# Two first-block mixers without accumulating weight transfers, and a second block whose gate columns run under its attention

## The chip, the core and the metric

The kernel runs on one core of a Trainium2 chip. Its engines are TensorE (PE, and PEld for its weight loads), VectorE (DVE), ScalarE (ACT), GpSimd (POOL) and SyncE (SP, which here only starts transfers). The metric is the device time of one execution in microseconds. Three runs of the kernel before took 3379.87, 3381.11 and 3383.58 us; the median is 3381.11 us.

## The reference

The program is two blocks in a row on one sequence of 1024 tokens of width 1024, in float32.

```
for i in range(2):                                   # first block
    hn = rmsnorm(h, norm1[i]);  z = hn @ w_in[i]
    u, (q, k, v) = z[:256], split(z[256:], 3)        # 12 heads of 64
    h = h + concat(pool_mixer(u), dilated_mixer(q, k, v)) @ w_out[i]
    h = h + square(relu(rmsnorm(h, norm2[i]) @ w_up[i])) @ w_down[i]
    h = h + sigmoid(rmsnorm(h, norm3[i]) @ w_gate[i]) * (p[i] @ w_ple[i])
x = rmsnorm(h, final_norm)

u = x @ w_in_2 + b_in_2                              # second block, 5632 columns
q, k, v, z_att, glu_a, glu_b, z_conv, g_att, g_conv = split(u)
att  = stick_breaking(q, k, v)                       # 8 heads of 64, causal
a_br = (att * silu(z_att)) @ w_att_proj
c    = silu(layer_norm(causal_conv31(glu_a * sigmoid(glu_b))))
c_br = (c * silu(z_conv)) @ w_conv_proj + b_conv_proj
y    = (sigmoid(g_att) * a_br + sigmoid(g_conv) * c_br) @ w_out_2
out  = layer_norm(2**0.25 * x + y)
```

The dilated mixer is attention in three groups of four heads with windows; stick-breaking attention needs, for every query, a running product over its keys.

## The kernel before, in words

Every product of two float32 matrices is made of three passes of reduced-precision matmuls: a matrix is held as a high part (`whi`, `xh`) and a low part (`wlo`, `xl`), and PE adds high times high, high times low and low times high (`mm_b`, L318, L320, L322; `project`, L502 to L504; `project_a`, L574 to L576). A weight tile of 128x1024 comes from memory into `wst` (SP queue, L213, a ring of three buffers) and is split in `split_w`. ACT copies it into `whi` (L294). The low part is made in one of two ways. With `by_dma` off, DVE subtracts: `wlo = wst - whi` (L299). With `by_dma` on, ACT writes `-whi` into `wlo` (L296) and a transfer on the POOL queue (L297) reads the weight from memory once more and adds it. In the kernel before, `by_dma` is on in the mixer of each of the first block's two layers (from the pooled columns to the first two output columns) and in the second block from the first keys on until the convolution is finished.

All weights come in the order of one list (`make_plan`); `stage` loads up to four entries ahead, `advance` splits up to two ahead. A "column" in what follows is one 128-wide output column of a 1024-deep product for all 1024 tokens: 8 slices of 6 matmuls with 512 columns, 48 matmuls.

Two streams of work run beside these columns as Python generators. After each slice `mm_b` calls `tick(1.3)`, after each two of `project` `tick(1.36)`, and a generator spawned with a period takes one step whenever so many ticks have gone by. The order of the instructions on each engine is fixed in this way when the program is built; each engine then works through its own queue in order.

In the first block's mixer the attention of a group (scores `S`, L666 and L669; exponentials `E` on ACT, L677; transposes `te`, L694, into `ET`; values `o`, L722 and L724) runs beside the projections of the next one. Queries and keys are rotated: DVE writes `sh` and `zq` or `za` (L516, L517), a small transfer on the POOL queue adds shifted rows (`za<-sh`, L519), ACT and DVE then make the key's parts `kS` (L543, L551).

In the second block, `stick` is the attention: 64 scores (4 head pairs, 4 blocks of queries, 2 heads, 2 halves) over 128 to 1024 keys. A score is matmuls `S` (L1352, L1354), a mask on DVE (L1357), sigmoids on ACT (L1358, L1359), a running product on DVE (L1361), and a product (L1362). Its weights are then transposed (`tw`, L1370), split (`wh` on ACT, `wl` on DVE, L1374) and multiplied with the values (L1389, L1391). `conv_all` is the convolution: 31 steps on DVE for each of four channel tiles (L1312, L1315), then a layer norm. `stick` has a period of 1.6 ticks, `conv_all` of 2.0. The columns beside them are the inputs of both, the gates of the attention branch (`gate(m)`, columns 28 to 35, whose sigmoids SP stores to `sad`), and `z_att` (12 to 15). Then come `w_att` with the stored gates fetched back on the POOL queue (`fetch_sa`) and `z_conv` (24 to 27), then `w_conv` with the gates of the convolution branch (36 to 43), one column in front of most of its eight halves, and the partial sums read back from `mgd`; last the output product `fin` (L1633).

Of the kernel before, what the change touches and what calls it, by code (L numbers as in the profile page):

```python
# [12 lines left out]
F32 = mybir.dt.float32  # L13
# [55 lines left out]
class K:  # L69
# [80 lines left out]
    def make_plan(self):  # L150
        p = []
        for i in range(DEPTH):
            p += [("w_u", i, 0), ("w_u", i, 1)]
            for g in range(3):
                for which in ((0, 1, 2) if g < 2 else (1, 0, 2)):
                    p += [("w_qkv", i, g, which, j) for j in range(2)]
            p += [("w_out", i, 0), ("w_out", i, 1), ("old", i, 0), ("old", i, 1)]
            for m in range(2, 8):
                p += [("w_out", i, m), ("old", i, m)]
            ups = [("w_up", i, m) for m in range(32)]  # L160
            p += ups[0:4]
            for c in range(8):
                if c < 7:
                    p.append(ups[4 * c + 4])
                p += [("w_down", i, c, mp) for mp in range(4)]
                p += ups[4 * c + 5:4 * c + 8]
            for m in range(8):
                if m == 4:
                    p.append(("w_ple", i, 1))
                p.append(("w_gate", i, m))  # L170
                if m == 1:
                    p.append(("w_ple", i, 0))
        w2 = lambda *cs: [("w_in2", c) for c in cs]
        wv = lambda c: [("w_v", c, 0), ("w_v", c, 1)]
        p += w2(20, 16, 0, 4, 1) + wv(0) + w2(5, 28, 21, 17, 29, 2, 6, 30, 22, 18, 31) + wv(1) + w2(3, 7, 32, 23, 19, 33)
        p += w2(12, 13, 14, 15, 34, 35)
        for m in range(8):
            if m % 2 == 0:
                p.append(("w_att", m // 2))
            if m % 2 == 1:  # L180
                p += w2(24 + m // 2)
        p += w2(36, 37)
        wo = lambda *ks: [("w_out2", k) for k in ks]
        for m in range(8):
            if 0 < m < 7:
                p += w2(37 + m)
            if m % 2 == 0:
                p.append(("w_conv", m // 2))
            p.append(("mg", m))
            p += {5: wo(0), 6: wo(1), 7: wo(2, 3, 4, 5, 6, 7)}.get(m, [])  # L190
        return p

    RAW = ("old", "mg", "w_out2")
# [197 lines left out]
    def setup(self):  # L391
        nc, a = self.nc, self.a
        self.ident = self.const("ident", [128, 128])
        nc.sync.dma_start(self.ident, a["c_ident"])
        self.ones = self.const("ones", [128, 2])
        nc.vector.memset(self.ones, 1.0)
        self.qlow = [self.const("ql%d" % n, [128, 512], F32R) for n in range(2)]
        self.qn = 0
        for x in self.qlow:
            nc.gpsimd.memset(x.bitcast(F32), 0.0)  # L400
        self.pinv = self.const("pinv", [128, 34])
        nc.gpsimd.dma_start(self.pinv, a["c_pinv"])
        self.pscale = self.const("pscale", [128, 4])
        nc.gpsimd.dma_start(self.pscale, a["pool_scale"])
        self.td = self.dram.tile([2, 128, 1024], F32, name="td")
        self.xd = self.dram.tile([8, 128, 1024], F32, name="xd")
        self.mgd = self.dram.tile([8, 128, 1024], F32, name="mgd")
        self.sad = self.dram.tile([8, 128, 1024], F32, name="sad")
        self.atd = self.dram.tile([4, 128, 1024], F32, name="atd")
        self.od = self.dram.tile([2, 2, 128, 1024], F32, name="od")  # L410
        self.yd = self.dram.tile([2, 128, 1024], F32, name="yd")
        self.sd1 = self.dram.tile([128, 64], F32, name="sd1")
        self.sd23 = self.dram.tile([128, 128], F32, name="sd23")
# [466 lines left out]
    def mixer(self, i, nm, h):  # L880
# [31 lines left out]
        if i == 0:  # L912
# [1 line left out]
            next(self.rot)  # L914
            self.defer(2.6, lambda: next(self.rot, None))
            tabs, self.tabs = self.tabs, None
        self.by_dma = True
        self.defer(3.9, start)
        if i > 0:
            for k in range(8):  # L920
# [118 lines left out]
        part(us, pss, order[4:6])  # L1039
        part(us, pss, order[6:8])  # L1040
        self.drop(2)
        self.by_dma = False
        for m in range(2):
            out(m, pss[m])
        for m in range(2, 8):
# [141 lines left out]
    def second(self, nm, h):  # L1187
# [15 lines left out]
        def lin(col):  # L1203
            ps = self.pair("l2")
            self.gemm(("w_in2", col,), box["xs"], ps)
            return ps, bcol[:, col:col + 1]
# [6 lines left out]
        def sig_of(ps, b):  # L1213
            t = self.st("sg")
            nc.scalar.activation(t, ps, AF.Sigmoid, bias=b)
            return t
# [39 lines left out]
        def gate(m):  # L1256
            t = sig_of(*lin(28 + m))
            nc.sync.dma_start(self.sad[m], t)

        def glu(sg, src, b):  # L1260
            nc.vector.scalar_tensor_tensor(sg, src, b, sg, OP.add, OP.mult)
            return sg

        cvs = [None] * 4
        cg = [None] * 4
# [40 lines left out]
        def conv_all():  # L1306
            for j in range(4):
                while cg[j] is None:
                    yield
                C, cg[j] = cg[j], True  # L1310
                acc = cvs[j] = self.st("cv")
                nc.vector.tensor_scalar(acc, C, cw[:, j, 30:31], cb[:, j:j + 1], OP.mult, OP.add)  # L1312
                yield
                for d in range(1, 31):
                    nc.vector.scalar_tensor_tensor(acc[:, d:1024], C[:, 0:1024 - d], cw[:, j, 30 - d:31 - d],  # L1315
                                                   acc[:, d:1024], OP.mult, OP.add)
                    yield
                C = None
            for _ in conv_norm():
                yield  # L1320
# [168 lines left out]
        self.by_dma = True  # L1489
        q1 = queries(*lin(1))  # L1490
        vs[0] = values(0)
        sk = self.spawn(stick(), 1.6)
        qk[1] = (q1, keys(*lin(5)))
        gate(0)
        ca = self.spawn(conv_all(), 2.0)
        cg[1] = glu(sig_of(*lin(21)), *lin(17))
        gate(1)
        qk[2] = (queries(*lin(2)), keys(*lin(6)))
        gate(2)
        cg[2] = glu(sig_of(*lin(22)), *lin(18))  # L1500
        gate(3)
        vs[1] = values(1)
        qk[3] = (queries(*lin(3)), keys(*lin(7)))
        gate(4)
        cg[3] = glu(sig_of(*lin(23)), *lin(19))
        gate(5)
        zs, ats, aT = [], [], []
        for j in range(4):
            zs.append(silu_of(*lin(12 + j)))
        self.finish(sk)  # L1510
        for j in range(3):
            aT.append(self.st("aT"))
# [5 lines left out]
            aT[j] = None  # L1518
            ats.append(self.split(zs[j], "at"))

        att(0)
        att(1)
        gate(6)
        att(2)
        att(3)
        gate(7)
        zc, sas = [], []

        def fetch_sa(m):
# [5 lines left out]
        for m in range(8):  # L1535
            if m % 2 == 0:
                u = self.take("w_att", m // 2)
            if m < 6:
                fetch_sa(m + 2)
            ps = self.pair("pt")  # L1540
            self.mm_b(self.halves(ps), self.wk(u, 4, (m % 2) * 512), ats)
            sa, sas[m] = sas[m], None
            nc.vector.tensor_tensor(sa, ps, sa, OP.mult)  # L1543
            nc.sync.dma_start(self.mgd[m], sa)
            if m % 2 == 1:
                self.drop()
                zc.append(silu_of(*lin(24 + m // 2)))

        zs = zc
        self.finish(ca)  # L1550
# [3 lines left out]
        for j in range(4):  # L1554
            nc.vector.tensor_tensor(zs[j], zs[j], cvs[j], OP.mult)
            cts.append(self.split(zs[j], "ct"))
        gs = [sig_of(*lin(36 + m)) for m in range(2)]
        mg, ms = [], []
        xrs = {}

# [21 lines left out]
        def split_m(k):  # L1582
# [1 line left out]
            mg[k] = None  # L1584

        before = {5: [(split_m, 0)], 6: [(split_m, 2), (split_m, 3)], 7: [(scale_x, 0), (scale_x, 1), (split_m, 5)]}
        after = {5: [(split_m, 1), (split_wo, 0)], 6: [(split_m, 4), (split_wo, 1)],
                 7: [(split_wo, 2), (split_m, 6), (split_wo, 3), (split_m, 7), (split_wo, 4), (split_wo, 5),
                     (split_wo, 6), (split_wo, 7)]}
        for m in range(8):  # L1590
            if 0 < m < 7:
                gs.append(sig_of(*lin(37 + m)))
            sc = gs.pop(0)
            if m % 2 == 0:
                u = self.take("w_conv", m // 2)
            old = self.take("mg", m)
            ps = self.pair("pc")
            self.mm_b(self.halves(ps), self.wk(u, 4, (m % 2) * 512), cts)
            if m % 2 == 1:
                self.drop()  # L1600
            if m == 4:
                fetch(0)
                fetch(1)
            if m == 6:
                box["xs"] = None
            for f, k in before.get(m, []):
                f(k)
            nc.vector.scalar_tensor_tensor(sc, ps, cb[:, 12 + m:13 + m], sc, OP.add, OP.mult)
            nc.vector.tensor_tensor(sc, sc, old, OP.add)
            mg.append(sc)  # L1610
            for f, k in after.get(m, []):
                f(k)
# [215 lines left out]
```

## Time and profile before

| What | Value |
|---|---|
| median of three runs | 3381.11 us |
| the profiled execution: time, span | 3376.4 us, 3374.6 us |
| PE busy | 3234.1 us (96%) |
| DVE, ACT, POOL busy | 1716.5, 1188.5, 253.9 us |
| mean granted TensorE clock | 0.986 of full speed |
| read from and written to memory | 216.09 MB, 30.08 MB |

The busy time of PE is that of a pipelined engine: it counts the time in which a matmul is under way, so short gaps and a slow start behind a wait are hidden in it. What a stretch could take at best is better counted in matmuls times the pace of a stretch without waits. The first layer's mixer lies between about 30 and 375 us, the second layer's between about 1280 and 1620 us; the second block begins at about 2510 us, its attention runs from about 2598 to 3025 us.

### The profile page before, as it was taken

The numbers are of one execution on the slowest core, as the hardware profiler recorded it, in microseconds if no ns is written. First come the engines' busy times: TensorE is split into PE (matmuls) and PEld (weight loads), VectorE is DVE, ScalarE is ACT, GpSimd is POOL, SyncE is SP. The second block draws the span as 40 slices with busy tenths as digits, with TensorE's granted clock in tenths as the row PEclk, the third lists the DMA queues.
The fourth block names the chain that finished last, engine by engine and source line by source line (L and its number), as shares of the span: only waits on it lengthen the run. The fifth ranks groups of instructions, "written<-read, shape, count | busy, mean of one in ns | idle before, by whom it ended". The sixth has DMA issues, their size and how long they took to land.

```text
span 3374.6 us, 38172 instructions
## 1 busy us (share of the span) xinstructions
PE 3234.1 (96%) x15596; PEld 2695.1 (80%) x15596; DVE 1716.5 (51%) x2518; ACT 1188.5 (35%) x1914; POOL 253.9 (8%) x344
## 2 busy tenths in 40 slices
PE   8898999999999999989999999999999888889998
PEld 7787788888888887878788888888888767678887
DVE  6545643333333545555543333333656888886345
ACT  4666421111111323666331111112334554543230
POOL 5122000000000002123000000000000000001000
PEclk9899999999999999989999999999999999999999
DMA  5243321111111114323321111112113323226331
GB/s 178 63 89 81 89 82 45 50 50 50 45 49 57 57 50 138 85 66 90 91 75 50 45 50 48 47 50 65 44 44 114 82 59 75 74 65 199 109 122 63
DMA packets 74222, 251.79 MB, mean 75 GB/s; under 512 B 11280, under 2 KB 11456, under 8 KB 74048
## 3 DMA queue, kind: packets, MB, share of 16 engines
q1 hardware_dynamic: 49248, 174.44, 16.0%
q0 software_dynamic: 23504, 70.46, 9.9%
q10 hardware_dynamic: 1296, 4.46, 0.3%
q8 instruction: 123, 2.02, 0.2%
q14 instruction: 51, 0.42, 0.0%
HBM read 216.09 MB, written 30.08 MB: 73 GB/s over the span
## 4 chain that ended last, share of the span: by engine, by line
PE 73%; DVE 14%; ACT 6%; DMA 3%; issue 3%; POOL 1%; DVEq 0%; ACTq 0%; POOLq 0%
PE pu L320 7%; PE pu L322 7%; PE pu L318 7%; PE pd L320 7%; PE pd L322 7%; PE pd L318 7%; DVE cv L1315 3%; PE fin L1633 3%; PE l L318 2%; PE l L320 2%; PE l L322 2%; PE pg L318 2%; PE pg L322 2%; PE pg L320 2%; DMA za<-sh 2%
## 5 line engine op out<-in xcount | busy, mean ns | idle before, releaser
L294 ACT ACTIVATE whi<-wst 128x1024 fp32r<-128x1024 f32 x258 | 271.0, 1051 | 650.0 <-PE pd L320 497.3
L318 PE MATMUL pu<-xh,whi 128*128 128x512 f32 x1088 | 336.7, 391 | 9.2 <-ACT xh L60 9.2
L1111 DVE TENSOR_TENSOR h<-pd,h 128x1024 f32<-128x1024 f32 x128 | 156.6, 1224 | 365.6 <-PE pd L322 365.4
L320 PE MATMUL pu<-xl,whi 128*128 128x512 f32 x1088 | 335.8, 390 | 0.9 <-DVE xl L61 0.9
L322 PE MATMUL pu<-xh,wlo 128*128 128x512 f32 x1088 | 335.4, 389 | 0.0
L320 PE MATMUL pd<-hidl,whi 128*128 128x512 f32 x1024 | 315.4, 389 | 0.5 <-DVE hidl L307 0.5
L322 PE MATMUL pd<-hidh,wlo 128*128 128x512 f32 x1024 | 315.3, 389 | 0.0
L318 PE MATMUL pd<-hidh,whi 128*128 128x512 f32 x1024 | 315.2, 389 | 0.0
L299 DVE TENSOR_TENSOR wlo<-wst,whi 128x1024 fp32r<-128x1024 f32 x184 | 224.0, 1221 | 50.2 <-ACT whi L294 50.2
L1066 DVE SCALAR_TENSOR_TENSOR hid<-pu,bc 128x1024 f32<-128x1024 f32 x62 | 75.9, 1225 | 339.1 <-PE pu L322 338.9
L318 PEld LDWEIGHTS pu<-xh,whi 128*128 128x128 f32 x1088 | 204.1, 188 | 51.5 <-ACT xh L60 9.6
L1067 ACT ACTIVATE hid<-hid 128x1024 f32<-128x1024 f32 x62 | 65.7, 1060 | 508.7 <-DVE hid L1066 508.7
L320 PEld LDWEIGHTS pu<-xl,whi 128*128 128x128 f32 x1088 | 204.4, 188 | 44.6 <-DVE xl L61 2.1
L322 PEld LDWEIGHTS pu<-xh,wlo 128*128 128x128 f32 x1088 | 204.5, 188 | 42.6
L320 PEld LDWEIGHTS pd<-hidl,whi 128*128 128x128 f32 x1024 | 192.0, 188 | 41.0 <-DVE hidl L307 1.3
L318 PEld LDWEIGHTS pd<-hidh,whi 128*128 128x128 f32 x1024 | 192.2, 188 | 40.0
L322 PEld LDWEIGHTS pd<-hidh,wlo 128*128 128x128 f32 x1024 | 192.2, 188 | 39.9
L318 PE MATMUL l<-nh,whi 128*128 128x512 f32 x576 | 188.0, 408 | 0.3 <-DVE sa L1543 0.3
L502 PE MATMUL pa<-xh,whi 128*128 128x512 f32 x448 | 185.4, 414 | 0.0
L503 PE MATMUL pa<-xl,whi 128*128 128x512 f32 x448 | 180.4, 403 | 0.0
L320 PE MATMUL l<-nl,whi 128*128 128x512 f32 x576 | 180.4, 394 | 0.0
L504 PE MATMUL pa<-xh,wlo 128*128 128x512 f32 x448 | 180.0, 402 | 0.0
(353 smaller groups left out, 6028.6 us busy)
## 6 DMA issues: line engine op xcount, KB each, us to landing
wst<-in_w_up_dram SPq DMA_DIRECT2D x64, 512.0 KB, 3.5
wst<-in_w_down_dram SPq DMA_DIRECT2D x64, 512.0 KB, 3.5
wst<-in_w_in_dram SPq DMA_DIRECT2D x40, 512.0 KB, 4.8
wst<-in_w_qkv_dram SPq DMA_DIRECT2D x36, 512.0 KB, 4.1
wlo<-in_w_qkv_dram POOLq DMA_DIRECT2D x32, 512.0 KB, 8.2
wlo<-in_w_in_dram POOLq DMA_DIRECT2D x29, 512.0 KB, 5.7
wst<-in_w_out_dram SPq DMA_DIRECT2D x24, 512.0 KB, 3.7
wst<-in_w_gate_dram SPq DMA_DIRECT2D x16, 512.0 KB, 3.7
```

Of the source, the lines that this page charges most:

```text
L294: nc.scalar.activation(h, w, AF.Copy)
L299: nc.vector.tensor_tensor(l, w, h.bitcast(F32), OP.subtract)
L318: mm(ps[h], wh, xh[:, h * 512:(h + 1) * 512], start=st, stop=False)
L320: mm(ps[h], wh, xl[:, h * 512:(h + 1) * 512], start=False, stop=False)
L322: mm(ps[h], wl, xh[:, h * 512:(h + 1) * 512], start=False, stop=sp)
L502: mm(out, wh, xh, start=k == 0, stop=False)
L503: mm(out, wh, xl, start=False, stop=False)
L504: mm(out, wl, xh, start=False, stop=k == 7)
L1066: nc.vector.scalar_tensor_tensor(t, ps, 0.0, box["bc"], OP.max, OP.mult)
L1111: nc.vector.tensor_tensor(h[m], ps, h[m], OP.add)
L1315: nc.vector.scalar_tensor_tensor(acc[:, d:1024], C[:, 0:1024 - d], cw[:, j, 30 - d:31 - d], acc[:, d:1024], OP.mult, OP.add)
L1633: nc.tensor.matmul(ps[e], xx[:, tok], ww[:, cs], start=False, stop=k == 7 and ww is wh and xx is ml, skip_group_check=True)
```

## The change

Two things are changed. In the mixers the switch `by_dma` stays off, so that the 38 weight tiles that were split there by ACT and an accumulating transfer are split by ACT and a subtraction on DVE. In the second block the columns stand in another order: the eight gate columns of the convolution branch are no longer computed inside the `w_conv` loop; seven of them (36 to 42) run beside or just behind the attention and are stored to `sad` like the others, the keys and queries of a head pair come later, `z_att` stands behind the attention, and the periods are 1.85 ticks for `stick` and 2.60 for `conv_all`.

```diff
@@ make_plan
-        p += w2(20, 16, 0, 4, 1) + wv(0) + w2(5, 28, 21, 17, 29, 2, 6, 30, 22, 18, 31) + wv(1) + w2(3, 7, 32, 23, 19, 33)
-        p += w2(12, 13, 14, 15, 34, 35)
+        p += w2(20, 16, 0, 4, 1) + wv(0) + w2(28, 21, 17, 29, 30, 31, 5, 32, 22, 18) + wv(1) + w2(2, 6, 33, 34, 35, 23, 19)
+        p += w2(3, 7, 36, 37, 38, 39, 40, 41, 12, 13, 14, 15, 42)
...
-            if 0 < m < 7:
-                p += w2(37 + m)
...
@@ mixer
-        self.by_dma = True
...
-        self.by_dma = False
@@ second
-        sk = self.spawn(stick(), 1.6)
+        sk = self.spawn(stick(), 1.85)
+        gate(0)
+        ca = self.spawn(conv_all(), 2.60)
+        cg[1] = glu(sig_of(*lin(21)), *lin(17))
+        for m in (1, 2, 3):
+            gate(m)
         qk[1] = (q1, keys(*lin(5)))
-        gate(0)
-        ca = self.spawn(conv_all(), 2.0)
...
-        gate(5)
+        for m in range(8, 14):
+            gate(m)
         zs, ats, aT = [], [], []
-        for j in range(4):
-            zs.append(silu_of(*lin(12 + j)))
         self.finish(sk)
...
-        att(0)
-        att(1)
-        gate(6)
-        att(2)
-        att(3)
-        gate(7)
+        for j in range(4):
+            zs.append(silu_of(*lin(12 + j)))
+            att(j)
+        gate(14)
...
-            if m < 6:
-                fetch_sa(m + 2)
+            fetch_sa(m + 2)
...
-        gs = [sig_of(*lin(36 + m)) for m in range(2)]
+        gs = sas[8:10]
+        g7 = sig_of(*lin(43))
...
         for m in range(8):
-            if 0 < m < 7:
-                gs.append(sig_of(*lin(37 + m)))
+            if m < 4:
+                fetch_sa(m + 10)
+                gs.append(sas[m + 10])
+            if m == 4:
+                fetch_sa(14)
+                gs += [sas[14], g7]
```

What the change does to the queues is seen at three places. First ACT in the first mixer, behind the first four exponentials of an attention group. Before:

```order
L677 ACTIVATE E,stat_378<-E,stat_378 128x128 x4
L294 ACTIVATE whi<-wst 128x1024
L296 ACTIVATE wlo<-whi 128x1024
L294 ACTIVATE whi<-wst 128x1024
L296 ACTIVATE wlo<-whi 128x1024
L650 ACTIVATE qS<-zq 64x256 x4
L543 ACTIVATE kS<-za 64x512 x2
```

Now, on ACT at the same place, and then on DVE at the same place:

```order
L675 ACTIVATE E,stat_378<-E,stat_378 128x128 x4
L292 ACTIVATE whi<-wst 128x1024 x2
L648 ACTIVATE qS<-zq 64x256 x4
L541 ACTIVATE kS<-za 64x512 x2
L675 ACTIVATE E,stat_378<-E,stat_378 128x256 x4
```

```order
L673 ISA E,stat_378<-S,bmasks 128x128
L673 ISA stat_378 128x1
L297 TENSOR_TENSOR wlo<-wst,whi 128x1024 x2
L651 SCALAR_TENSOR_TENSOR ql_142<-zq,qS 64x256 x2
L549 TENSOR_TENSOR kS<-za,kS 64x512 x2
```

Two copies have left ACT's queue in front of the queries `qS`, and two subtractions stand in DVE's queue in front of the queries' low part `ql`.

Second DVE in the second block, between two of the longest scores of the first head pair (`S` the mask, `fP` the running product, `be` the product, `cv` steps of the convolution). Before:

```order
L1357 TENSOR_TENSOR S_18136<-S_18136,smask 128x128
L1361 SCALAR_TENSOR_TENSOR fP<-fP 128x1024
L1362 TENSOR_TENSOR be<-be,fP 128x1023
L1315 SCALAR_TENSOR_TENSOR cv<-sg,n_16975,cv 128x1017
L1374 TENSOR_TENSOR wl<-tw,wh 128x384
L1315 SCALAR_TENSOR_TENSOR cv<-sg,n_16975,cv 128x1016
L1357 TENSOR_TENSOR S_18177<-S_18177,smask 128x128
```

Now:

```order
L1353 TENSOR_TENSOR S_18128<-S_18128,smask 128x128
L1357 SCALAR_TENSOR_TENSOR fP<-fP 128x1024
L1358 TENSOR_TENSOR be<-be,fP 128x1023
L1311 SCALAR_TENSOR_TENSOR cv<-sg,n_16937,cv 128x1012
L1370 TENSOR_TENSOR wl<-tw,wh 128x384
L1353 TENSOR_TENSOR S_18179<-S_18179,smask 128x128
```

One convolution step has gone from between these two scores; the longer periods leave fewer of them between scores on average and more matmuls of columns on PE.

Third SP's queue around the `w_conv` loop (`mgd` the stored partial sums, `w_in` a gate column, `w_out` the output weights). Before:

```order
L213 DMA wst<-mgd 128x1024
L213 DMA wst<-in_w_in_dram 128x1024
L213 DMA wst<-mgd 128x1024
L213 DMA wst<-in_w_in_dram 128x1024
L213 DMA wst<-in_w_conv_dram 128x1024
L213 DMA wst<-mgd 128x1024
L213 DMA wst<-in_w_in_dram 128x1024
L213 DMA wst<-mgd 128x1024
```

Now:

```order
L1537 DMA mgd<-sa 128x1024 x4
L211 DMA wst<-mgd 128x1024 x2
L211 DMA wst<-in_w_conv_dram 128x1024
L211 DMA wst<-mgd 128x1024 x2
L211 DMA wst<-in_w_conv_dram 128x1024
L211 DMA wst<-mgd 128x1024 x2
```

The loads of the partial sums and of `w_conv` follow each other without the weights of a gate column between them.

## Rows read from the trace of the kernel before

**Rows 1.** The page, part 1: busy time of each engine.
```profile
PE 3234.1 (96%) x15596; PEld 2695.1 (80%) x15596; DVE 1716.5 (51%) x2518; ACT 1188.5 (35%) x1914; POOL 253.9 (8%) x344
```
**Rows 2.** Busy time by stretch: length, PE, PEld, DVE, ACT, POOL, clock, DMA share, GB/s.
```profile
480.00:520.00 40.00, 40.00 (x178) 33.12 (x177) 17.28 (x16) 13.92 (x14) 0.00 (x0) 1.00 0.14 45
...
80.00:400.00 320.00, 286.71 (x1679) 248.32 (x1678) 178.45 (x473) 192.43 (x448) 67.75 (x94) 0.95 0.34 80
...
1320.00:1640.00 320.00, 291.91 (x1696) 252.40 (x1696) 175.53 (x470) 189.46 (x445) 69.48 (x97) 0.94 0.34 79
...
2598.00:3047.00 449.00, 397.47 (x2077) 324.33 (x2078) 384.92 (x488) 236.25 (x449) 23.35 (x28) 0.98 0.30 72
...
3047.00:3265.00 218.00, 217.69 (x969) 179.60 (x968) 95.51 (x96) 61.60 (x60) 14.51 (x19) 1.00 0.45 131
```
**Rows 3.** PE's waits over the whole span: us in total, times, longest.
```profile
PE S L666 <- ACT E L677: 19.5, 4, 5.6
PE te L694 <- DVE ET L704: 11.0, 6, 2.8
PE S L666 <- DVE kS L551: 10.1, 10, 5.4
```
**Rows 4.** ACT in order of time before one wait for E: start, us, instruction.
```profile
1445.84 1.04 ACT L294 ACTIVATE whi<-wst 128x1024 fp32r<-128x1024 f32 x1
1446.92 1.06 ACT L296 ACTIVATE wlo<-whi 128x1024 fp32r<-128x1024 f32 x1
...
1449.92 1.72 ACT L650 ACTIVATE qS<-zq 64x256 fp32r<-64x256 f32 x4
```
**Rows 5.** DVE at the same place, in order of time.
```profile
1450.36 0.42 DVE L653 SCALAR_TENSOR_TENSOR ql<-zq,qS 64x256 fp32r<-64x256 f32 x1 [8.60 <-ACT qS L650]
```
**Rows 6.** The chain that ended last, first mixer: start, us, what.
```profile
75.52 1.78 POOL wlo L297
77.36 6.68 DMA za<-sh
...
88.32 2.38 DMA za<-sh
```
**Rows 7.** PE by form, 2575 to 3050 us: busy, mean ns, idle before.
```profile
L318 PE MATMUL l<-nh,whi 128*128 128x512 f32 x368 | 123.4, 417 | 0.0
...
L1370 PE MATMUL tw<-ident,be 128*128 128x128 f32 x208 | 33.6, 281 | 21.1 <-ACT be L1359 9.8 <-DVE wl L1374 7.7 <-DVE aT L1400 2.9
```
**Rows 8.** DVE by form, 2575 to 3050 us.
```profile
L1374 DVE TENSOR_TENSOR wl<-tw,wh 128x512 fp32r<-128x512 f32 x48 | 32.9, 686 | 3.9 <-ACT wh L1373 3.6
...
L1361 DVE TENSOR_TENSOR_SCAN fP<-fP 128x1024 f32<-128x1024 f32 x8 | 18.3, 2292 | 5.3 <-ACT fP L1358 5.3
...
L1361 DVE TENSOR_TENSOR_SCAN fP<-fP 128x640 f32<-128x640 f32 x8 | 11.9, 1493 | 2.8 <-ACT fP L1358 2.8
...
L1362 DVE TENSOR_TENSOR be<-be,fP 128x1023 f32<-128x1023 f32 x8 | 9.8, 1225 | 0.8
...
L1362 DVE TENSOR_TENSOR be<-be,fP 128x639 f32<-128x639 f32 x8 | 6.6, 825 | 0.8
...
L1315 DVE SCALAR_TENSOR_TENSOR cv<-sg,n,cv 128x1010 f32<-128x1010 f32 x4 | 5.1, 1264 | 0.0
```
**Rows 9.** DVE in order of time: masks of a head pair's eight long scores.
```profile
2731.58 0.29 DVE L1357 TENSOR_TENSOR S<-S,smask 128x128 f32<-128x128 f32 x1
...
2776.31 0.28 DVE L1357 TENSOR_TENSOR S<-S,smask 128x128 f32<-128x128 f32 x1
```
**Rows 10.** The page, part 5: DVE subtractions for low parts, whole span.
```profile
L299 DVE TENSOR_TENSOR wlo<-wst,whi 128x1024 fp32r<-128x1024 f32 x184 | 224.0, 1221 | 50.2 <-ACT whi L294 50.2
```
**Rows 11.** Transfers by line: KB each, median us from issue to landing.
```profile
sa<-sad POOLq DMA_DIRECT2D x8, 512.0 KB, 9.8
...
wst<-mgd SPq DMA_DIRECT2D x8, 512.0 KB, 3.5
```
**Rows 12.** PE waits of a mixer's late transposes, in order of time.
```profile
315.12 0.63 PE L694 MATMUL te<-ident,E 128*128 128x128 f32 x4 [2.78 <-DVE ET L704]
```

More of the change, by code (lines that the diff above doesn't have):

```diff
@@ L179, in make_plan @@
                 p.append(("w_att", m // 2))
-            if m % 2 == 1:
-                p += w2(24 + m // 2)
-        p += w2(36, 37)
+            if 0 < m < 5:
+                p += w2(23 + m)
+        p += w2(43)
         wo = lambda *ks: [("w_out2", k) for k in ks]
         for m in range(8):
-            if 0 < m < 7:
-                p += w2(37 + m)
             if m % 2 == 0:
@@ L189, in make_plan @@
             p.append(("mg", m))
-            p += {5: wo(0), 6: wo(1), 7: wo(2, 3, 4, 5, 6, 7)}.get(m, [])
+            p += {6: wo(0), 7: wo(1, 2, 3, 4, 5, 6, 7)}.get(m, [])
         return p
@@ L407, in setup @@
         self.mgd = self.dram.tile([8, 128, 1024], F32, name="mgd")
-        self.sad = self.dram.tile([8, 128, 1024], F32, name="sad")
+        self.sad = self.dram.tile([15, 128, 1024], F32, name="sad")
         self.atd = self.dram.tile([4, 128, 1024], F32, name="atd")
@@ L1491, in second @@
         vs[0] = values(0)
-        sk = self.spawn(stick(), 1.6)
+        sk = self.spawn(stick(), 1.85)
[4 more added lines that the diff above has]
+            gate(m)
         qk[1] = (q1, keys(*lin(5)))
-        gate(0)
-        ca = self.spawn(conv_all(), 2.0)
-        cg[1] = glu(sig_of(*lin(21)), *lin(17))
-        gate(1)
+        gate(4)
+        cg[2] = glu(sig_of(*lin(22)), *lin(18))
+        vs[1] = values(1)
         qk[2] = (queries(*lin(2)), keys(*lin(6)))
[L1499 to L1502, printed above, removed]
+        for m in (5, 6, 7):
+            gate(m)
+        cg[3] = glu(sig_of(*lin(23)), *lin(19))
         qk[3] = (queries(*lin(3)), keys(*lin(7)))
-        gate(4)
-        cg[3] = glu(sig_of(*lin(23)), *lin(19))
-        gate(5)
+        for m in range(8, 14):
+            gate(m)
         zs, ats, aT = [], [], []
-        for j in range(4):
-            zs.append(silu_of(*lin(12 + j)))
         self.finish(sk)
@@ L1546, in second @@
                 self.drop()
-                zc.append(silu_of(*lin(24 + m // 2)))
+            if 0 < m < 5:
+                zc.append(silu_of(*lin(23 + m)))
         zs = zc
@@ L1586, in second @@
         before = {5: [(split_m, 0)], 6: [(split_m, 2), (split_m, 3)], 7: [(scale_x, 0), (scale_x, 1), (split_m, 5)]}
-        after = {5: [(split_m, 1), (split_wo, 0)], 6: [(split_m, 4), (split_wo, 1)],
-                 7: [(split_wo, 2), (split_m, 6), (split_wo, 3), (split_m, 7), (split_wo, 4), (split_wo, 5),
+        after = {5: [(split_m, 1)], 6: [(split_m, 4), (split_wo, 0)],
+                 7: [(split_wo, 1), (split_wo, 2), (split_m, 6), (split_wo, 3), (split_m, 7), (split_wo, 4), (split_wo, 5),
                      (split_wo, 6), (split_wo, 7)]}
         for m in range(8):
-            if 0 < m < 7:
-                gs.append(sig_of(*lin(37 + m)))
+            if m < 4:
[4 more added lines that the diff above has]
+                gs += [sas[14], g7]
             sc = gs.pop(0)
```

## The prediction

> **What bounds the kernel now.** I read the busy times first: PE is busy for 96% of the span and the next engine for 51% [rows 1]. That makes PE the engine whose work sets the time, but not at its best everywhere, so the next view is busy time by stretch. In a stretch of the first MLP PE never waits: 178 matmuls in 40 us, 0.2247 us each, at a granted clock of 1.00, which is 2.4 GHz [rows 2]. One column of 48 matmuls is then 10.8 us. The change removes no matmul. What it can give is only time in which PE waits or starts slowly, and that lies in three stretches: the two mixers (33 and 28 us without a matmul in 320 us each) and the attention of the second block, 2598 to 3047 us (51.5 us without one) [rows 2]. From 3047 to 3265 us PE is busy to 0.3 us [rows 2].
>
> In the attention stretch the busy time hides more. PE's need there: 23 columns (368 matmuls in each of the three passes [rows 7]), 248 us; the products for the second half of the values, 192 matmuls half as wide, 22 us; the attention's own work. Scores and values each move 64 scores' worth, 73,728 columns of moving data, which at 0.2247 us for 512 is 32 us for either, and 288 transposes at about 0.11 us (half a 256-wide matmul's pace, an estimate) are 31 us. Together 366 us in 449 us: 83 us are lost. DVE is busy for 385 of the 449 us [rows 2], so it is the engine that PE waits for. The gaps between long scores show how: the masks of one head pair's eight long scores lie 6.39 us apart on average (44.73 us over 7) [rows 9]. In such a gap DVE has the mask 0.29 us, the running product 1.89 us and the product 1.03 us (means of the longest and the shortest form), a split `wl` 0.69 us, and, with two attention steps of 1.6 ticks and a convolution step each 2.0 ticks, 1.6 convolution steps of 1.26 us, 2.0 us [rows 8, 9]; with about 0.2 us for queries and sums that is 6.1 us, 95% of the gap. PE needs 3.2 ticks of columns, 3.2/1.3 times 6 matmuls, 3.3 us, and some 1.6 us of attention: 4.9 us. So PE loses 1.5 us at each of 32 long scores, 48 of the 83 us.
>
> **The change in the second block.** Seven gate columns of the convolution branch come into the stretch, and 76 us leave the loops behind it. The stretch then needs 442 us of PE. DVE's work in it stays about the same, because sigmoids of gates are ACT's. With 1.85 and 2.60 ticks a gap of two attention steps holds 3.7/1.3 times 6 matmuls, 3.85 us, and the 1.6 us of attention: 5.45 us for PE; DVE has 1.42 convolution steps, 1.8 us, and 5.9 us in all. At the same 95% the gap takes 6.2 us, and PE loses 0.75 us instead of 1.5: 24 us saved over 32. The other 35 us (short scores, ends of head pairs, waits for the clock) I lower by the ratio of what PE has to do in a gap, to about 25. So 83 us of loss become 48: minus 35 us. The bounds: nothing, if the loss stays whatever stands beside it, and 83 us, if PE never waits. A worse loss than before has no row for it: no DVE work is added there, and the later keys only hold up the attention, beside which gate columns run.
>
> **The w_conv loop.** It loses its gate columns, and 8 halves of 24 matmuls take 43 us. With column 43 in front, 54 us must cover what comes in: 8 partial sums, 3 tiles of `w_conv`, 5 stored gates, some 4 of `w_out`, 2 of x, 22 transfers of 512 KB, 11.5 MB, 213 GB/s. The stretch had 131 GB/s [rows 2]. Behind the ring of three buffers a partial sum's load waits for the sum two halves earlier and has 10.8 us less two DVE steps; a load takes 3.5 us there, but a fetch of a gate behind others on POOL took 9.8 us [rows 11]. I take plus 3 us. The near bound is 0; the far one is the loop at the rate of [rows 2], 11.5 MB at 131 GB/s, 88 instead of 54 us, plus 34. The same DVE chain that ends the convolution (four products, four splits at about 3.5 us each, 15 us behind the last `w_att`) now has 10.8 us of one column as its cover instead of two columns; the halves use the four tiles 1.35 us apart, which leaves at most 1 us of this, within the 3.
>
> **The mixers.** Each of the two loses 19 negated copies on ACT (1.06 us [rows 4]) and 19 transfers, and gains 19 subtractions on DVE at 1.22 us [rows 10], 46 us of DVE in all. DVE is busy 178 and 176 of 320 us there [rows 2].
>
> First, the waits for E: 4 times, 19.5 us in all [rows 3]. Before each of them ACT works through two tiles, `whi` and `wlo` twice, from 1445.84 to 1449.92, and the queries, whose low part DVE needs, come behind that [rows 4]; DVE has stood idle for 8.60 us at that point [rows 5], so two subtractions, which can begin when the first `whi` is there, end before `ql` can start. ACT comes to the queries 2.1 us earlier and the whole chain to E moves by that: 4 times 2.1, minus 8.4 us. Second, in each mixer the late transposes wait for the split `ET`, 2.78 us in the first [rows 12], 11.0 us over 6 waits [rows 3]; two tiles' copies stand in front of it on ACT, and in the order of now the two subtractions in front of it on DVE, which leave 1.7 of the 2.1 us: minus 3.4 us for both mixers. Third, the rotations' small transfers shared the POOL queue with the accumulating ones: behind two of them `za<-sh` was issued late (POOL 1.78 us) and took 6.68 us, where it takes 2.38 us otherwise [rows 6]. The key's parts then come 4 us or more earlier, but PE is still busy with its projection at that time, so that only the part of the 10.1 us of waits for kS [rows 3] that hangs on DVE's order goes: I take 1.2 us in each mixer and 0.8 us for later rotations, minus 4 us. Together minus 16 us. The bounds: all three kinds of waits gone, minus 40.6 us, and all subtractions in the path, 38 times 1.22, plus 46 us.
>
> What is queued behind the added wait: a subtraction waits for its `whi`, and `ql`, `ET`, `vS` or `kS` behind it on DVE wait too, and then PE. I see it covered in all ten places but expect no gain in six of them. The weight buffer is held until DVE has read it, some 2 to 5 us longer; loads run four entries ahead, a group of two tiles lasts over 20 us, and a load takes under 5 us.
>
> **The sum.** 3376.4 (the profiled execution) minus 35 minus 16 plus 3 is 3328.4 us. That execution lies 4.7 us under the median of the runs shown, so against the median I predict 3333 us.
>
> **Rivals.**
> - All of PE's loss in the attention goes: minus 83 instead of minus 35, 3285 us. For it: PE's need and DVE's are nearly equal in a long gap now. Against: the row of steps from score to scan to transposes stays, and DVE's 5.9 us still lie above PE's 5.45.
> - The attention's loss stays at 83 us because it is the chain's and not the load's: 3368 us. For it: DVE is at 86% over the stretch, not at 100% [rows 2]. Against: 95% in the long gaps.
> - The `w_conv` loop is held by its transfers, plus 34 instead of plus 3: 3364 us. For it: nothing stands between the loads any more, and fetched gates came in 9.8 us [rows 11]. Against: each gate is asked for two halves ahead.
> - Slower: DVE sets the pace in the mixers. Each pair of subtractions, 2.44 us plus the wait for the second `whi`, comes ahead of work that PE waits for; if all 38 reach PE, plus 46 us instead of minus 16: 3395 us. It decides from the point where DVE's idle time before the pair is under 2.4 us. Before `ql` it is 8.60 us [rows 5], and DVE is busy for just over half the mixer, so I give it little. The Trainium skill (Perfetto Trace Analysis, Optimizing Scalar/DVE Operations) advises moving work from a saturated DVE to ScalarE, the opposite of this edit. By that rule the edit would cost up to these 46 us; the trace has DVE at 56% and ACT at 60% of the mixer, so its condition isn't met here.
>
> **Chances.** The forecast 0.70, with 3305 to 3357 us as its own range; no loss left 0.08; loss unchanged 0.07; loop held by transfers 0.09; slower through DVE 0.06. The range of 3300 to 3366 us takes in the forecast's range, most of the loop's case and part of the second. No change is within 0.2% (6.8 us), about what a measurement of this kernel can tell. All cases but the last lie clearly below 3374 us; a part of the last and the edges of two others fall within 0.2%: faster 0.92, same 0.03, slower 0.05.
>
> **What would show it.** In the changed profile: the waits of S for E fall from about 5 us to about 3; no `za<-sh` takes 6 us; DVE is busier by some 22 us in each mixer and ACT less by 20. From the first score to the first `w_att` matmul about 490 us pass instead of 449, with 30 columns in them; the gap between long scores is near 6.2 us. From there to the end of the `w_conv` loop it is about 145 us instead of 218 (seven columns less), with less than 5 us of waits. The prediction is wrong if that stretch stays longer than 155 us, if PE in the mixers waits for `wlo` or for a later `ql`, or if the gaps between long scores stay at 6.4 us or fall to 5.5.

## The result and the profile after

The changed kernel takes 3331.4 us (median of 4 runs, 3328.1 to 3333.9), the kernel before on the same chip 3380.6 us: a ratio of 0.985, 95% interval 0.984 to 0.987. I predicted 3333 us. The total came out; how it is made up did not. I split 48 us into 35 for the attention of the second block, 16 for the mixers and 3 given back in the `w_conv` loop. The traces put 18.8 us into the attention, 29.5 into the mixers, 0.9 into the loop, and 4.5 given back behind it: 44.7 us between the two profiled executions. The other 4.5 of the 49 us lie in which execution was profiled: that of the kernel before took 3376.4 us, 4.2 under its median. Two errors of 13 to 16 us cancelled each other, which is luck, and most of what follows is on them.

The page's busy times, which answer to [rows 1]:

```profile
PE 3220.8 (97%) x15596; PEld 2689.7 (81%) x15596; DVE 1755.4 (53%) x2550; ACT 1156.0 (35%) x1882; POOL 227.1 (7%) x319
```

PE executes as many matmuls as before and is busy 13.3 us less with them. Since the matmuls are the same, I take most of that for time in which they ran at the lower clock; the rows of the mixers below bear this out. DVE's busy time rises by 38.9 us and ACT's falls by 32.5. The 38 subtractions of the mixers are 46 us, but the second block has 6 fewer than before: six more of its tiles are split while `by_dma` is on.

The mixers first. These rows show busy time by stretch (length, then PE, PEld, DVE, ACT, POOL, then PE's granted clock, DMA share, GB/s), each stretch from one place in the work (the first matmuls of `pa` for one mixer) to another (the last transpositions of its output begin). Before:

```profile
75.10:372.95 297.85, 264.57 (x1580) 230.11 (x1578) 163.44 (x458) 181.18 (x436) 71.53 (x99) 0.94 0.36 81
1302.00:1618.68 316.68, 288.60 (x1679) 249.44 (x1678) 179.18 (x482) 188.65 (x448) 81.44 (x112) 0.94 0.36 83
```

After:

```profile
75.04:355.59 280.55, 259.21 (x1587) 225.09 (x1585) 179.41 (x471) 165.24 (x421) 55.88 (x81) 0.98 0.20 55
1284.60:1587.74 303.14, 281.98 (x1680) 243.50 (x1678) 198.85 (x499) 170.51 (x431) 66.30 (x96) 0.98 0.21 58
```

The same work takes 17.3 and 13.5 us less. PE's time without a matmul falls from 33.3 and 28.1 us to 21.3 and 21.2, by 18.9 together; its busy time falls by 5.4 and 6.6, by 12.0 together, and the mean clock rises from 0.94 to 0.98. Two kinds of gain stand beside each other here: waits that are gone, and matmuls that no longer run at 1.2 GHz behind a wait. Read microsecond by microsecond, 84 of them lie below full clock in the two stretches before, and 29 after.

PE's waits over the whole span (us in total, times, longest), to be read against [rows 3]:

```profile
PE te L692 <- DVE ET L702: 12.3, 8, 3.3
...
PE S L664 <- ACT E L675: 10.6, 4, 4.0
...
PE fin L1622 <- issue: 3.1, 1, 3.1
...
PE S L664 <- DVE kS L549: 0.4, 1, 0.4
```

The waits for E fall from 19.5 to 10.6 us, the waits for kS from 10.1 to 0.4. The waits for ET, which I had expected to shrink, grow by 1.3. Another row of before is gone:

```profile
PE S L666 <- DVE stat L675: 5.3, 2, 2.7
```

The second block by stretch, cut at the first score, the first `w_att` matmul, the first matmul of the last projection and the end. Before:

```profile
2598.40:3047.20 448.80, 397.67 (x2078) 324.52 (x2079) 384.72 (x487) 236.06 (x448) 22.95 (x28) 0.98 0.30 72
3047.20:3270.00 222.80, 222.49 (x990) 183.50 (x989) 100.27 (x100) 63.44 (x62) 14.51 (x19) 1.00 0.44 130
3270.00:3374.60 104.60, 94.64 (x449) 78.49 (x447) 61.00 (x163) 14.19 (x14) 5.30 (x6) 0.97 0.31 106
```

After:

```profile
2568.90:3074.40 505.50, 469.98 (x2414) 392.25 (x2415) 399.59 (x496) 260.17 (x469) 31.16 (x39) 0.98 0.36 87
3074.40:3220.80 146.40, 146.37 (x654) 120.38 (x653) 77.74 (x82) 46.43 (x45) 14.43 (x21) 1.00 0.62 185
3220.80:3329.90 109.10, 95.76 (x449) 78.27 (x447) 64.27 (x166) 15.12 (x15) 5.31 (x6) 0.98 0.33 111
```

The first score comes 29.5 us earlier. The attention stretch is 56.7 us longer and holds seven more columns, 336 matmuls, which at 0.2247 us each [rows 2] are 75.5 us of work: a gain of 18.8. The loops behind it lose exactly these 336 matmuls, are 76.4 us shorter, run at 185 GB/s and never wait. The tail is 4.5 us longer, 3.1 of it in one wait.

### The profile page after: what moved, and what is told of

Its sections match the earlier page's. It is cut to its first block, busy times and chain, and to the rows that moved or that the text cites. A ratio compares the mean times of both kernels' runs of the same rounds, so it can differ in the third digit from the quotient of the medians.

```text
span 3329.9 us, 38203 instructions
## 1 busy us (share of the span) xinstructions
PE 3220.8 (97%) x15596; PEld 2689.7 (81%) x15596; DVE 1755.4 (53%) x2550; ACT 1156.0 (35%) x1882; POOL 227.1 (7%) x319
## 4 chain that ended last, share of the span: by engine, by line
PE 75%; DVE 12%; ACT 5%; issue 3%; DMA 2%; POOL 0%; DVEq 0%; ACTq 0%; POOLq 0%
PE pu L318 7%; PE pu L320 7%; PE pu L316 7%; PE pd L318 7%; PE pd L320 7%; PE pd L316 7%; PE l L318 2%; PE l L316 2%; PE l L320 2%; DVE cv L1311 2%; PE fin L1632 2%; PE pg L316 2%; PE pg L320 2%; PE pg L318 2%; PE po L316 2%
## 5 line engine op out<-in xcount | busy, mean ns | idle before, releaser
L297 DVE TENSOR_TENSOR wlo<-wst,whi 128x1024 fp32r<-128x1024 f32 x216 | 261.4, 1220 | 70.0 <-ACT whi L292 69.7
L320 PE MATMUL l<-nh,wlo 128*128 128x512 f32 x576 | 179.6, 393 | 0.0
```

Of the source, the lines that this page charges most:

```text
L297: nc.vector.tensor_tensor(l, w, h.bitcast(F32), OP.subtract)
L320: mm(ps[h], wl, xh[:, h * 512:(h + 1) * 512], start=False, stop=sp)
```

## The experiments

Times are medians, ratios are to the kernel before in the same comparison (3379.6 to 3380.8 us), intervals are 95%.

**The two halves alone.** `e1_mixers_only` takes the two `self.by_dma` lines out of the mixers of before; `e2_second_only` is the changed kernel with them put back:

```
-        self.by_dma = True
         self.defer(3.9, start)
...
         self.drop(2)
-        self.by_dma = False
```

> The kernel before with the mixers' part of the change alone; the second block is that of before. Theory A (read off the changed kernel's trace: the last transposes of the two mixers come 17.4 and a further 13.6 us earlier, since every wait that goes takes a stretch of TensorE at 1.2 GHz with it): about 31 us faster than before, 3350 us. Theory B (the split in the prediction, waits at their own length alone): 16 us faster, 3364 us. Under both the second block takes as long as before, 773 to 776 us from its first score to the end.

> The changed kernel with the mixers of before (negated copies and transfers); only the second block is changed. Theory A: 14 to 17 us faster than before, 3364 to 3366 us. Theory B (the prediction: 35 less in the attention, 3 more in the w_conv loop): 32 us faster, 3349 us. The gains of this and of the mixers alone should add up to the 49 us of the whole.

Measured: 3345.2 us (0.990, 0.988 to 0.991) and 3365.2 us (0.996, 0.994 to 0.997): 35 and 15 us, 50 together, as the whole change gives 49. The split of the trace holds and that of the prediction does not. The mixers seem to give 5 us more than the 29.5 I read off, but the difference is again the profiled execution: between those of before (3376.4 us) and of e1 (3347.2 us) lie 29.2 us.

**The mixers' edit in two.** `e3_add_on_DVE` keeps ACT's negated copy and replaces the transfer; `e4_copy_on_DVE` keeps the transfer and takes the copy from ACT. Both stand on the kernel before.

```
e3:  nc.scalar.activation(l, h.bitcast(F32), AF.Copy, scale=-1.0)
-    nc.gpsimd.dma_start(l, self.source(key), accum_op=OP.add)
+    nc.vector.tensor_tensor(l, w, l.bitcast(F32), OP.add)
e4:
-    nc.scalar.activation(l, h.bitcast(F32), AF.Copy, scale=-1.0)
+    nc.vector.tensor_scalar(l, h.bitcast(F32), -1.0, None, OP.mult)
     nc.gpsimd.dma_start(l, self.source(key), accum_op=OP.add)
```

> The kernel before, in whose mixers only the transfers are replaced: ScalarE still makes the negated copy, and VectorE adds the weight to it. Theory T (the transfers on the queue of the rotations were the larger cost): the wait of 5.39 us for kS and those named stat go, the waits for E stay at 4 to 5.6 us: 18 to 25 us faster than before, 3356 to 3362 us. Theory S (ScalarE's copies were the larger cost, as the prediction split it: 11.8 of 16): about 4 to 8 us faster, 3373 to 3377 us.

> The kernel before, in whose mixers only the negated copy moves from ScalarE to VectorE; the accumulating transfers stay. Theory T: the waits for E fall to about 4 us or less, the wait of 5.39 us for kS stays: 8 to 13 us faster than before, 3368 to 3373 us. Theory S: 12 us by the waits alone and some 20 with the clock, 3360 to 3368 us. The za<-sh of over 6 us behind two transfers stays under both.

Measured: 3373.6 us (0.998, 0.997 to 0.999) and 3365.9 us (0.995, 0.994 to 0.997), 6.5 and 14 us faster, 21 together where both at once give 35. By time theory S is right. The waits show that each cause has its own. PE's waits in e3:

```profile
PE S L669 <- ACT E L680: 22.0, 4, 6.0
...
PE te L697 <- ACT qS L653: 5.9, 2, 2.9
...
PE S L669 <- DVE kS L554: 0.8, 2, 0.4
```

and in e4:

```profile
PE S L669 <- ACT E L680: 11.9, 4, 3.4
...
PE S L669 <- DVE kS L554: 9.1, 8, 5.4
...
PE S L669 <- DVE stat L678: 5.4, 2, 3.2
```

Without the transfers the waits for kS are nearly gone and those for stat halve (2.7 us in e3); without ACT's copy the waits for E fall to 12. The transfer's way to PE is the rotation: in the chain that ended last, `za<-sh` took 6.68 us behind two accumulating transfers [rows 6], and after the change

```profile
82.57 2.42 DMA za<-sh
...
89.51 2.40 DMA za<-sh
```

The halves do not add up: 14 us come only with both. In e3 half of the edit builds a worse chain, and in e4 the waits for kS and stat stay; that these two account for all of the 14 us is not shown. In e3 DVE's additions wait for ACT's second copy and stand ahead of `ql`, in order of time on DVE:

```profile
99.48 1.23 DVE L298 TENSOR_TENSOR wlo<-wst,wlo 128x1024 fp32r<-128x1024 f32 x1 [8.11 <-ACT wlo L296]
101.51 1.23 DVE L298 TENSOR_TENSOR wlo<-wst,wlo 128x1024 fp32r<-128x1024 f32 x1 [0.81 <-ACT wlo L296]
102.66 0.86 DVE L656 SCALAR_TENSOR_TENSOR ql<-zq,qS 64x256 fp32r<-64x256 f32 x2
```

The second addition ends as `ql` begins, so the waits for E rise from 19.5 to 22.0 us and a new wait for qS appears.

**What a subtraction costs.** `e5_double_wlo` does the subtraction twice for `w_qkv` and `w_out`; `e9_no_wlo` leaves it out for them (`return h, h` behind ACT's copy), so that the low parts of these weights are missing from the result.

> The changed kernel, with each of the 38 subtractions in the first block's mixers done twice (46 us more of VectorE). Theory C (VectorE has room nearly everywhere; only the subtractions right ahead of ql and ET reach TensorE): the four waits for E and the late ones for ET grow by 1.2 to 2.4 us each, with the clock 8 to 18 us slower than the changed kernel, 3339 to 3350 us. Rival (VectorE sets the pace, the prediction's slower case): all 38 reach TensorE, 46 us slower or more, 3377 us and up.

> The changed kernel without the 38 subtractions in the first block's mixers: the high parts of these weights stand in for the low ones in the third product, so the low parts are left out of the result, and TensorE's work is the same. Doubling the subtractions cost 39 us. Theory L (each costs the same, about 1 us, whether it is the first or the second): 30 to 39 us faster than the changed kernel, 3292 to 3302 us. Theory K (the first one mostly finds VectorE idle, the second fills what is left): 5 to 15 us faster, 3316 to 3326 us.

Measured: 3370.4 us (0.997, 0.996 to 0.998), 39 us slower than the changed kernel, and 3315.3 us (0.981, 0.979 to 0.983), 16 us faster. Both edits reach further than the 38 subtractions that the expectations name: `w_qkv` and `w_out` have 52 tiles in the first block. The row of the second subtraction in e5:

```profile
L299 DVE TENSOR_TENSOR wlo<-wst,whi 128x1024 fp32r<-128x1024 f32 x52 | 63.7, 1225 | 1.8
```

Ten of the 14 others stand in the output columns behind the mixers and cost nothing there: in the first layer PE's 300 matmuls from the 1951st on take 68.0 us in the changed kernel, in e5 and in e9 alike. So the price falls on the other 42, some 51 us of work on DVE, which cost 16 us the first time and 39 the second. For the doubling, theory C (8 to 18 us) fell, and the rival (all of them, 46 us or more) is not reached. For leaving them out, K is nearer, one microsecond outside its range: the price is not the same for the first and the second. The waits in e5, for ET and E:

```profile
PE S L666 <- ACT E L677: 24.0, 4, 6.5
PE te L694 <- DVE ET L704: 17.5, 8, 4.4
```

and in e9:

```profile
PE te L695 <- DVE ET L705: 11.6, 8, 3.0
...
PE S L667 <- ACT E L678: 6.8, 4, 2.2
```

From none to one to two subtractions the waits for E go 6.8, 10.6, 24.0 us, those for ET 11.6, 12.3, 17.5. The first subtraction already reaches E: the chain that ended last, followed back through the first of these waits after the change (start, us, what), runs through it,

```profile
96.25 0.96 ACT whi L292
...
97.27 1.11 issue
98.37 1.06 DVE wlo L297
...
99.51 0.41 DVE ql L651
```

and `ql` begins only as the second subtraction ends. In e9, without subtractions, the same chain comes to `ql` straight from ACT's queries:

```profile
93.00 0.42 ACT qS L651
...
93.44 0.43 DVE ql L654
```

**The second block: where the values stand.** The trace after, cut to the long scores of the four head pairs (from the first to the last mask of eight; columns as above):

```profile
2600.50:2645.80 45.30, 40.87 (x200) 33.23 (x200) 40.04 (x46) 23.46 (x47) 1.73 (x2) 0.96 0.27 58
2712.70:2768.40 55.70, 46.51 (x282) 40.95 (x281) 45.17 (x58) 24.46 (x53) 2.31 (x3) 0.89 0.19 41
2840.60:2884.00 43.40, 40.52 (x206) 33.02 (x205) 38.35 (x45) 25.57 (x51) 2.60 (x3) 1.00 0.44 108
2955.40:2999.00 43.60, 39.54 (x192) 31.95 (x191) 38.33 (x44) 24.79 (x49) 2.12 (x3) 0.96 0.36 86
```

Three pairs lose 4.4, 2.9 and 4.1 us without a matmul; before, each of the four lost about 7.5, as the second and third did:

```profile
2731.60:2776.30 44.70, 37.25 (x186) 28.72 (x185) 40.44 (x47) 25.87 (x52) 1.72 (x2) 1.00 0.28 71
2851.70:2898.90 47.20, 39.67 (x194) 29.78 (x192) 42.99 (x49) 27.00 (x53) 1.77 (x2) 1.00 0.14 23
```

The second pair after the change loses 9.2 us and has the lowest clock: the second half of the values, which stood between pairs, now runs there in place of columns. DVE's 12 further instructions there are the values' own (`vx`, `vT`), 5.1 us, and PE's waits there name them beside the splits `wl`:

```profile
PE S L1348 <- DVE wl L1370: 4.0, 3, 2.2
PE S L1348 <- DVE vx L1243: 2.3, 3, 1.3
```

`e6_values_later` moves it (the weights' plan follows):

```
-        vs[1] = values(1)
+        gate(5)
         qk[2] = (queries(*lin(2)), keys(*lin(6)))
-        for m in (5, 6, 7):
+        vs[1] = values(1)
+        for m in (6, 7):
```

> The changed kernel with the second half of the values moved from beside the long scores of the second head pair to behind the third pair's keys; the gate column 5 takes its place. Theory V (that place is what the second block lost against the prediction: 9.19 us without a matmul there against 2.9 to 4.4 in the other pairs, and three stretches at 1.2 GHz that cost some 9 us): 6 to 12 us faster than the changed kernel, 3319 to 3325 us. Rival (the values' work holds the attention up wherever it is put): within 3 us of it, 3328 to 3334 us, with the idle time in the third pair's short scores.

Measured: 3319.2 us (0.982, 0.981 to 0.984), 12 us faster than the changed kernel; theory V. The second pair's long scores now read

```profile
2712.90:2758.50 45.60, 42.27 (x209) 34.54 (x207) 40.07 (x46) 25.14 (x50) 2.60 (x3) 0.96 0.35 81
```

with 3.3 us without a matmul, like the others. The edit also brings the keys of the third pair and a gate column forward; that is not separated from the values' place.

**Periods and order.** `e7_old_periods` is the changed kernel with `stick` at 1.6 and `conv_all` at 2.0; `e10_old_order_longer` is e1 with 1.7 and 2.2; `e11_values_later_195` is e6 with 1.95 for `stick`. The order of before with the full 1.85 and 2.60 was not run, so that the periods alone are tried at four tenths of their step.

> The changed kernel with the old periods, 1.6 for the attention's steps and 2.0 for the convolution's. Theory P (the columns that stand in a gap between long scores fill TensorE's idle time, so fewer of them lose it again): the four long stretches go back from 4 to 7 us without a matmul each, 8 to 15 us slower than the changed kernel, 3339 to 3346 us. Rival (the new order of columns carries the gain): within 3 us of it.

> The mixers' part alone (3345 us), with the second block's column order of before and periods of 1.7 and 2.2 instead of 1.6 and 2.0; that order cannot go as far as 1.85 and 2.60. Theory P (the periods carry the gain by themselves; in the new order the whole step was worth 30 us): four tenths of it, 8 to 12 us faster than the mixers alone, 3333 to 3337 us. Rival (periods and order only work as a pair, since longer periods need columns that stand beside the attention): within 4 us of the mixers alone, 3341 to 3349 us.

> The kernel with the values moved (3319 us), with a period of 1.95 instead of 1.85 for the attention's steps. Theory P: fewer steps beside each column leave TensorE less idle time in the gaps, 4 to 8 us faster, 3311 to 3315 us. Rival (what is left are waits inside one attention item, which the period does not change): within 3 us, 3316 to 3322 us.

Measured: 3360.9 us (0.995, 0.993 to 0.996), 30 us slower than the changed kernel; 3340.8 us (0.988, 0.987 to 0.990), 4 us faster than e1; 3312.1 us (0.980, 0.978 to 0.981), 7 us faster than e6. The stretch from first score to first `w_att` matmul in e7, e10, e6 and e11, each row from its own trace:

```profile
2567.50:3111.20 543.70, 488.97 (x2442) 399.37 (x2443) 427.11 (x535) 268.89 (x478) 31.76 (x39) 0.96 0.34 81
```

```profile
2567.30:3005.00 437.70, 395.26 (x2078) 327.69 (x2079) 372.89 (x477) 237.15 (x448) 23.08 (x29) 0.97 0.31 74
```

```profile
2569.00:3063.90 494.90, 464.19 (x2415) 386.49 (x2416) 398.70 (x497) 259.80 (x469) 31.32 (x39) 0.99 0.37 89
```

```profile
2568.90:3056.20 487.30, 461.24 (x2415) 384.84 (x2416) 398.44 (x496) 259.11 (x469) 31.24 (x39) 1.00 0.38 91
```

The new order with old periods has 54.7 us without a matmul instead of 35.5, and 19.0 us more busy time at clock 0.96 (28 matmuls of the convolution's layer norm come into the stretch): theory P in direction, twice the upper end of its size. The long scores of the four pairs lose 7.8, 13.6, 4.9 and 6.2 us, the second again worst. The kernel is 16 us slower than the old order with the old periods (e1, 3345): the new order alone is a loss. Which part of it (later keys, the values' place, the gates) makes the loss was not separated. In the old order longer periods shorten the stretch by 11 us, but give part of it back behind: a wait that e1 does not have appears ahead of the `w_conv` loop,

```profile
PE pc L318 <- ACT sg L1213: 4.6, 1, 4.6
```

since the convolution now ends too late for it, 14 us later than in e1 (its last step on DVE at 3109.4 against 3095.3 us). So, as far as these runs go, periods and order carry the gain as a pair; the 4.3 us of e10 lie at the edge of its rival's 4, and well under theory P's 8 to 12. In e11, with the new order, longer still is better; PE's time without a matmul falls to 26.1 us. That version beats both kernels, by 69 us and 19 us.

**The tail.** I took the wait of 3.1 us in the last projection to be for the second tile's PSUM buffer. `e8_last_product_first` lets the last product on DVE come before a split of `w_out` and one of the products' splits:

```
-  7: [(scale_x, 0), (scale_x, 1), (split_m, 5)]}
+  7: [(scale_x, 0), (scale_x, 1)]}
...
-  6: [(split_m, 4), (split_wo, 0)], 7: [(split_wo, 1),
+  6: [(split_m, 4)], 7: [(split_wo, 0), (split_m, 5), (split_wo, 1),
```

> The changed kernel; on VectorE the product of the last w_conv half comes ahead of the first split of w_out and one of the products' splits, which stood before it. Theory F (the wait of 3.15 us ahead of the second tile of the last projection is for the PSUM buffer that this product frees): that wait falls to under 1 us, 1 to 3 us faster than the changed kernel. Rival (the split of w_out is late instead): no gain, with a wait for wlo in its place.

Measured: 3333.0 us (0.986, 0.984 to 0.988), the same as the changed kernel. PE's waits there:

```profile
PE fin L1632 <- ACT woh L1573: 2.3, 1, 2.3
...
PE fin L1632 <- DVE wlo L297: 0.8, 1, 0.8
...
PE fin L1622 <- issue: 0.6, 1, 0.6
```

The named wait went, as theory F has it, and 3.1 us of others took its place: the rival is right on the time.

## Why the prediction was right in its total and wrong in its parts

**Mixers, minus 16: measured minus 29.5 in the traces, 35 by medians.** The waits for E came out in their sum only: 8.4 us expected, 8.9 found. Each was to shrink by 2.1 us; the four of 5.1, 3.7, 5.6 and 5.1 us became 4.0, 0.7, 4.0 and 1.9. The step "two subtractions, which can begin when the first `whi` is there, end before `ql` can start" is wrong: the chain behind the change runs through the second of them, and without them (e9) the waits for E are 3.8 us shorter. The step for ET (minus 3.4) failed in its sum, plus 1.3. The wait that I had read, 2.78 us [rows 12], did shrink by about the 1.7 us named, but an earlier one, 2.4 us before, grew in both mixers, and two new ones of 1.4 and 0.6 us came; after, in the first mixer,

```profile
246.34 0.63 PE L692 MATMUL te<-ident,E 128*128 128x128 f32 x4 [3.33 <-DVE ET L702]
...
297.31 0.63 PE L692 MATMUL te<-ident,E 128*128 128x128 f32 x4 [0.95 <-DVE ET L702]
```

The subtractions are not the main reason, since without them (e9) the waits for ET still sum to 11.6 us. I had left out that PE, held up less before, comes to the next wait sooner; the waits for stat, 2.7 us just ahead of the ones that grew, are gone. That this is the cause is argued, not shown.

The step for the rotations (minus 4) was too small by more than half: I argued that PE is still busy with its projection when the key's parts arrive, but of the 10.1 us of waits for kS 9.7 went, and 5.3 named stat with them; e4, where the transfers stay, still has 9.1 and 5.4 of these. Last, I priced a wait at its own length. PE's busy time in the mixers fell by a further 12.0 us, since behind a removed wait the matmuls no longer run at the lower clock. That term was missing altogether, though [rows 2] had the clock at 0.95 and 0.94 in the mixers against 1.00 in the MLP.

**Attention, minus 35: measured minus 18.8.** The working on the long gaps (1.5 us of loss each become 0.75) holds in its ratio for three head pairs, 7.5 us over seven gaps become 2.9 to 4.4, about half. I applied it to all four. The move of the values under the second pair's long scores stood in the changed order, and I had priced their 22 us of PE work but not their place: their DVE work (58 instructions there against 46 in the first pair) falls into the gaps in which DVE is the engine that PE waits for. Undoing that place gives 12 us, which would have made it minus 31; the last 4 us are not accounted for.

**`w_conv` loop, plus 3.** The rival of a loop held by its transfers did not occur: 146.4 us, 0.03 of it without a matmul, at 185 GB/s. I had expected 145 and set 155 as the bound of being wrong. What was given back stands behind it, 4.5 us in the tail, where I looked for nothing; e8 moves 3.1 us of it from one wait to others and gains nothing.

**The slower rival.** DVE as the engine that sets the mixers' pace decided nothing at one subtraction, but it was nearer than I gave it credit: the work costs 16 us as it stands, and the same amount again cost 39. The stretches 75 to 400 and 1320 to 1640 us of e5 have DVE busy for 431 of 645 us:

```profile
sum 645.00, PE 582.23 PEld 504.07 DVE 431.21 ACT 344.80 POOL 116.46; mean PE 291.12 PEld 252.04 DVE 215.60 ACT 172.40 POOL 58.23
```

The Trainium skill (Perfetto Trace Analysis, Optimizing Scalar/DVE Operations) ties its advice to take work off DVE to DVE being saturated. In these runs DVE work cost time well before that: on the way to 67% each further microsecond of it cost about 0.76 (39 of some 51).

**The signs named.** DVE plus 22 in each mixer and ACT minus 20: over the same work plus 16 and 20, and minus 16 and 18. No `za<-sh` over 6 us: seen. Gaps of 6.2: 6.2 in two pairs, 6.5 and 8.0 in the others, so that in two of four pairs the gaps did not fall under 6.4, which I had named as a sign of being wrong; a later `ql` in the mixers, another such sign, was there too. 490 us from first score to `w_att`: 505.5.

**What stays open.** Which instruction put off the waits for stat was not followed, nor what makes up the 14 us by which e3 and e4 together fall short of both at once.

## What to carry to other kernels

When a wait goes, read the granted clock of the stretch behind it as well: here 19 us of waits took 12 us of slow matmuls with them. Price work on the engine that others wait for by where it stands in that engine's queue, not by its busy share; the same 51 us cost 16 at first and 39 the second time. When an order changes, look for the one block that lands where the waiting engine is already late, and test it by moving that block alone.

## What the runs showed of the hardware

A small transfer behind two accumulating ones on the same POOL queue took 6.68 us and 2.4 us without them. Matmuls behind a wait of 5.39 us ran at half the clock for several microseconds: the stretch of the first mixer around that wait in the kernel before has a granted clock of 0.57 on average,

```profile
87.00:99.00 12.00, 6.54 (x21) 5.30 (x22) 5.23 (x15) 2.46 (x4) 4.60 (x6) 0.57 0.16 18
```

with the microseconds from 88 to 98 in it at 0.50, which is 1.2 GHz. Summed over both mixers the stretches below full clock, read by single microseconds, were 14 before and 6 after.
